# Sums of w_out's quarters: built a chunk of all four quarters at a time, stored from the sync queue

## The chip, the cores and the metric

The kernel runs on one core of one Trainium2 chip. The metric is the device time of one execution, in microseconds. The kernel before takes 1799.5 us (median of 3 runs, 1798.72 to 1800.11).

## The reference, cut to what matters

One decoder layer over 1024 positions of width 2048. After an RMSNorm and one input projection the columns split in two groups, and both groups' results meet in one output projection:

```
proj = rms_norm(x, norm_w) @ w_in
# group A: 8 heads x 128, gated delta rule in chunks of 64 (state recurrence)
# group B: 8 channel groups x 128, u * (W_s LN(v) + b) in chunks of 128, times silu(z)
mix = concatenate([o_a, o_b], -1) @ w_out        # (1024 x 2048) @ (2048 x 2048)
out = rms_norm(x + mix, final_norm_w)
```

The change concerns only how operands of the last product, `@ w_out`, are prepared.

## The kernel before, in words

The positions are worked in two halves of 512 (`hf` 0 and 1). In each half `group_a` projects eight heads in four pairs and runs the delta rule on them, and `group_b` projects v in three blocks of 256 columns (the `vb` matmuls, L790) and then u and z of eight channel groups (sixteen calls of `project`, 48 matmuls each: `acc`, L239 to L242). After both halves `out_phase` does the output projection. Every matmul operand is split in a high and a low part (`split`, L135 on ACT and L136 on DVE), so that three matmuls stand for one.

The output projection is done by a seven-product scheme of fast matrix multiplication on 2 x 2 blocks: `PRODUCTS` lists for each product which quarters of the left operand and of `w_out` are added. For products 0, 2 and 6 (`SUMS`) the sum or difference of two quarters of `w_out` is made beforehand, by `w_sums`, while group B runs, and kept in the DRAM tile `wc_d`; `out_phase` loads it from there. A quarter is 1024 x 1024, and is handled in chunks of 128 x 512 (256 KB): 2 column blocks `cb` by 8 row blocks `k` (`HK` is 8). So there are 3 x 16 = 48 sums in all. The first half makes the first 24 (all of product 0, and product 2 for `cb` 0), the second half the other 24.

`w_sums` makes one sum at a time: two loads issued by SP (`wsa` L839 into a buffer of tag `cv`, of which there are 3; `wsb` L840 into one of tag `bv`, of which there are 2), one DVE operation (L847), and one store issued by POOL (L848).

Two things set the order of the work. First, `w_sums` and most tasks of the heads are generators that are put on a list by `spawn` and advanced by `tick`, which the projections call after every six matmuls of 512 columns or twelve of 256. `yield n` lets n ticks pass. This gives the order in which instructions are written down. A call of `group_b` has 176 ticks: 48 in the three `vb` blocks and 128 in the sixteen projections. `w_sums` is spawned when group B's first weights are requested, four chunks of weights ahead of their matmuls and so about 8 ticks before the first of them. Second, the language then schedules the written instructions: it lays out each engine's queue before the program runs, by its own estimates of durations, with the order of writing as priority. An instruction whose inputs and buffers the estimate sees as free can be put in its queue well ahead of ones that are written before it. On the chip each queue runs in its fixed order, and an instruction at its head that waits holds those behind it.

Other places that the prediction's steps touch:

- The last pair of heads of a half (pair 3) finishes inside group B. Its state recurrence (`read` and `write`, L622 to L634) needs PE, DVE and PE again in turn. Then, one head after the other, come `at` (L650, PE), `o` (L651, DVE), a row of small operations, a scaling on POOL (L662), and a transposition through DRAM issued by POOL: four stores `swapo<-ut` (L431) and one load `ut<-swapo` (L434). The result is used at L673 on DVE, which frees a buffer of tag `ut`.
- `spatial` (L745, PE) fills one of the two PSUM banks of tag `gen`; L747 on DVE empties it into a buffer `s` of tag `ut`, of which there are 2. The `at` of the pair's second head needs a `gen` bank too.
- `w_chunk` issues the load of each weights chunk from SP (L186), into one of 3 buffers; its split parts have 4 buffers.

Of the kernel before, what the change touches and what calls it, by code (L numbers as in the profile page):

```python
# [8 lines left out]
F32 = mybir.dt.float32  # L9
# [3 lines left out]
ALU = mybir.AluOpType  # L13
# [4 lines left out]
P = 128  # L18
DM = 2048
SEQ = 1024  # L20
T = 512
# [10 lines left out]
def kernel(ctx, tc, x_tok, x_t, w_in, w_v0, w_vb, w_out, conv_w, norm_w, a_log, dt_bias,  # L32
                       hn_w, sgu_w, sgu_b, wsp_t, b_sp, fn_w, out):
    nc = tc.nc
# [5 lines left out]
    wk = pool("wk", bufs=2)  # L40
# [4 lines left out]
    def proj_bank(name):  # L45
        return ps.tile([P, T], F32, tag="proj", bufs=3, name=name)
# [71 lines left out]
    wc_d = dr.tile([3, 2, KT // 2, P, T], F32, name="wc_d", bufs=1)  # L118
# [64 lines left out]
    def w_chunk(src, shape, name, keep=None, raw=None, add=None):  # L183
        if raw is None:
            raw = wp.tile(shape, F32, tag="wr", bufs=3, name=f"wr{name}")
        nc.sync.dma_start(raw, src)  # L186
        if add:
            nc.vector.tensor_tensor(raw, raw, add[0], op=add[1])
        hi, lo = keep or (wp.tile(shape, F32R, tag="wh", name=f"wh{name}"), wp.tile(shape, F32R, tag="wl", name=f"wl{name}"))
        split(hi, lo, raw)  # L190
        return hi, lo
# [7 lines left out]
    def spawn(gen):  # L199
        n = next(gen, None)  # L200
        if n is not None:
            tasks.append([n, gen])

    def tick():
        for t_ in list(tasks):
            t_[0] -= 1
            if t_[0] <= 0:
                n = next(t_[1], None)
                if n is None:
                    tasks.remove(t_)  # L210
                else:
                    t_[0] = n
# [37 lines left out]
    def project(hf, ct, xs, done):  # L250

        st = {}
        for q in range(KT // KH):
            def mm(w, q=q):
                if q == 0:
                    st["acc"] = proj_bank(f"acc{hf}_{ct}")
                mm_chunk(st["acc"], w, xs, q)
                if q == KT // KH - 1:
                    done(st["acc"])
                    tick()  # L260
            yield (lambda q=q: w_tile(hf, ct, q)), mm
# [56 lines left out]
    def vsl(vn, t, c0, c1):  # L318

        return vn[c0 // T][:, t, c0 % T:c0 % T + c1 - c0]  # L320
# [135 lines left out]
    W_GATES = 12  # L456
    W_LN = 12
    W_EM = 5
    W_SUM0 = 18

    def task_k(hf, h, st, pr, acc):
        gt, hh = st["gt"], h % 2
# [255 lines left out]
    def task_ln(hf, vn, stt, sb):  # L718

        mv = sm.tile([P, NT, 2], F32, tag="mv", name=f"mv{hf}")  # L720
        rv = sm.tile([P, NT], F32, tag="rv", name=f"rv{hf}")
        va = sm.tile([P, NT], F32, tag="va", name=f"va{hf}")
        r4 = rstd[:, hf * NT:(hf + 1) * NT]
        for t in range(NT):
            nc.vector.bn_aggr(mv[:, t, :], stt[:, t])
        nc.vector.tensor_tensor(va, mv[:, :, 1], r4, op=ALU.mult)
        nc.vector.tensor_tensor(va, va, r4, op=ALU.mult)
        nc.vector.tensor_scalar(va, va, EPS, None, op0=ALU.add)
        rsqrt_(rv, va, [P, NT], f"v{hf}")
        nc.vector.tensor_tensor(rv, rv, r4, op=ALU.mult)  # L730
        for t in range(NT):
            v = vsl(vn, t, 0, T)
            nc.vector.tensor_scalar(v, v, mv[:, t, 0:1], rv[:, t:t + 1], op0=ALU.subtract, op1=ALU.mult)
        for t in range(NT):
            v = vsl(vn, t, T, 2 * T)
            nc.vector.tensor_scalar(v, v, mv[:, t, 0:1], rv[:, t:t + 1], op0=ALU.subtract, op1=ALU.mult)
        yield W_LN
        for g in range(2):
            spatial(hf, vn, sb, g)
            yield 1  # L740
# [12 lines left out]
    def task_u(hf, g, sb, acc):  # L753
        while g not in sb:
            yield 1
        nc.vector.tensor_tensor(sb[g], sb[g], acc, op=ALU.mult)

    def task_zb(hf, g, vn, sb, acc):
        za = scaled(acc, sb["rb"], f"zb{hf}_{g}")
        z = wk.tile([P, T], F32, tag="z", bufs=2, name=f"zb{hf}_{g}")  # L760
        nc.scalar.activation(z, za, AF.Silu)
        mx = wk.tile([P, T], F32, tag="kc", bufs=2, name=f"mb{hf}_{g}")
        nc.vector.tensor_tensor(mx, sb[g], z, op=ALU.mult)
        nc.sync.dma_start(mix_d[hf][H + g], mx)
        yield 1
        if g + 2 < NG:
            spatial(hf, vn, sb, g + 2)

    def group_b(hf, xs, st):

        env, sb = {}, {}
        units = [(n, cb, k) for n in SUMS for cb in range(2) for k in range(HK)]
        spawn(w_sums(units[hf * len(units) // 2:(hf + 1) * len(units) // 2]))
        for blk in range(1, 4):
            for k2 in range(KT // 2):
                def mm(w, blk=blk, k2=k2):
                    hi, lo = w
                    if blk == 1 and k2 == 0:
                        sb["rb"] = st["rb"]
                        env["vn"] = st["vn"] + [big.tile([P, NT, T], F32, tag="b8", name=f"vn{hf}_1")]  # L780
                    if k2 == 0:
                        env["acc"] = [proj_bank(f"vb{hf}_{blk}_{i}").rearrange("p (t c) -> p t c", c=256) for i in range(2)]
                    acc, vn = env["acc"], env["vn"]
                    for k in (2 * k2, 2 * k2 + 1):
                        xh, xl = xs[k]
                        for t in range(NT):
                            a, tsl = acc[t // 2][:, t % 2, :], slice(t * P, (t + 1) * P)
                            first, last = k == 0 and t % 2 == 0, k == KT - 1
                            for l, r, fl, sp_ in ((xh, hi, first, False), (xh, lo, False, False), (xl, hi, False, last)):
                                nc.tensor.matmul(a, l[:, tsl], r[:, k % 2, :], start=fl, stop=sp_, skip_group_check=True)  # L790
                        if k % 2 == 0:
                            tick()
                    if k2 == KT // 2 - 1:
                        for t in range(NT):
                            v = vsl(vn, t, blk * 256, (blk + 1) * 256)
                            nc.scalar.copy(v, acc[t // 2][:, t % 2, :])
                            nc.vector.bn_stats(st["st"][:, t, blk, :], v)
                        if blk == 3:
                            spawn(task_ln(hf, vn, st["st"], sb))
                    tick()  # L800
                yield (lambda blk=blk, k2=k2: w_chunk(w_vb[blk - 1, k2], [P, 2, 256], f"vb{hf}_{blk}_{k2}")), mm
        for g in range(NG):
            yield from project(hf, 4 * H + g, xs, lambda acc, g=g: spawn(task_u(hf, g, sb, acc)))
            yield from project(hf, 5 * H + g, xs, lambda acc, g=g: spawn(task_zb(hf, g, env["vn"], sb, acc)))
# [4 lines left out]
    HK = KT // 2  # L809
    PRODUCTS = (  # L810
# [7 lines left out]
    )  # L818


    SUMS = (0, 2, 6)
# [4 lines left out]
    op = {1: ALU.add, -1: ALU.subtract}  # L826

    def w_quarter(b, cb, k):

        return w_out[b[1] * 2 + cb, b[0] * HK + k]  # L830

    def w_sums(units):

        def load(u):
            n, cb, k = u
            a, b, _ = PRODUCTS[n][1]
            ta = wk.tile([P, 1, T], F32, tag="cv", bufs=3, name=f"wsa{n}_{cb}_{k}")
            tb = wk.tile([P, 1, T], F32, tag="bv", bufs=2, name=f"wsb{n}_{cb}_{k}")
            nc.sync.dma_start(ta, w_quarter(a, cb, k))  # L839
            nc.sync.dma_start(tb, w_quarter(b, cb, k))  # L840
            return ta, tb
        yield W_SUM0
        nxt = load(units[0])
        for i, (n, cb, k) in enumerate(units):
            (ta, tb), nxt = nxt, (load(units[i + 1]) if i + 1 < len(units) else None)
            yield 6
            nc.vector.tensor_tensor(ta, ta, tb, op=op[PRODUCTS[n][1][2]])  # L847
            nc.gpsimd.dma_start(wc_d[SUMS.index(n), cb, k], ta.rearrange("p o c -> p (o c)"))  # L848

    def out_phase():  # L850

# [209 lines left out]
```

## Time and profile before

| | |
|---|---|
| median of 3 runs | 1799.5 us |
| the profiled execution's own time | 1797.79 us |
| its span, first to last instruction | 1796.1 us |
| mean granted TensorE clock | 0.99 of full speed |
| PE busy | 1731.5 us, 96% of the span |
| DVE busy | 1271.1 us, 71% |
| ACT busy | 734.2 us, 41% |
| POOL busy | 290.2 us, 16% |
| moved by DMA | 284.27 MB, 158 GB/s over the span |

PE is the matmul engine. Its busy time bounds the kernel, so what another engine does costs time only where PE stands still for it, or runs at a lower granted clock after standing still. The stages follow each other: group A of the first half ends near 455 us, its group B near 735 us, group A of the second half near 1191 us, its group B near 1455 us, and the rest is the output projection.

### The profile page before, as it was taken

Reading aid. Unit: us, or ns where it says so; the run is one execution under the profiler, and the core shown is the slowest. Engines: PE = TensorE matmul, PEld = TensorE weight load, DVE = VectorE, ACT = ScalarE, POOL = GpSimd, SP = SyncE. Lnnn points to the kernel's source line nnn. Section 1 sums busy time; section 2 is a strip of 40 time slices with the busy share of each in tenths; the row PEclk is TensorE's granted clock in tenths of the full one; section 3 lists DMA queues with packets and bytes.
Section 4 is the critical chain, followed back from the end, with each engine's and each line's share of the span. In section 5 each row is a group of like instructions: output and inputs, shape, how many; then the busy total and the mean of one; then the engine's idle time right before and its main releaser. Section 6 shows DMA issues by size and latency. Waiting matters only on the chain.

```text
span 1796.1 us, 27540 instructions
## 1 busy us (share of the span) xinstructions
PE 1731.5 (96%) x9334; PEld 1458.4 (81%) x9334; DVE 1271.1 (71%) x2985; ACT 734.2 (41%) x1670; POOL 290.2 (16%) x362
## 2 busy tenths in 40 slices
PE   9999999999999799999999999999889999999997
PEld 8778787887997688887888888889778888778876
DVE  7798787987746633758879889793664345777885
ACT  7543544444333222636344444532422233333463
POOL 3210121211202300202012122120131000100121
PEclk9999999999999899999999999999999999999999
DMA  7455454364458744426453645443884367656774
GB/s 233 130 134 142 106 135 132 94 175 118 135 180 276 237 118 124 127 61 172 128 135 91 167 106 147 133 120 111 271 277 139 105 187 235 193 162 193 217 235 147
DMA packets 190429, 284.27 MB, mean 158 GB/s; under 512 B 38448, under 2 KB 71248, under 8 KB 190032
## 3 DMA queue, kind: packets, MB, share of 16 engines
q1 hardware_dynamic: 181760, 257.30, 49.8%
q0 software_dynamic: 8384, 25.21, 4.7%
q8 instruction: 73, 1.20, 0.3%
q14 instruction: 68, 0.56, 0.1%
q10 hardware_dynamic: 144, 0.01, 0.0%
HBM read 233.12 MB, written 49.32 MB: 157 GB/s over the span
## 4 chain that ended last, share of the span: by engine, by line
PE 66%; DVE 14%; DMA 11%; issue 4%; ACT 3%; POOL 1%; SPq 1%; DVEq 0%; ACTq 0%; POOLq 0%
PE acc L239 13%; PE acc L242 12%; PE acc L240 12%; PE vb L790 7%; PE oa L983 4%; PE oa L982 4%; PE oa L981 4%; DVE wl L136 2%; DMA wsb<-w_out 2%; DVE cv L414 2%; DMA xres<-x_tok 2%; DMA wc_d<-wsa 2%; DMA ar<-mix_d 1%; DMA pc<-swapk 1%; DVE fs L569 1%
## 5 line engine op out<-in xcount | busy, mean ns | idle before, releaser
L239 PE MATMUL acc<-xh,wh 128*128 128x512 f32 x1472 | 592.3, 402 | 1.0 <-ACT wh L135 1.0
L242 PE MATMUL acc<-xh,wl 128*128 128x512 f32 x1472 | 578.4, 393 | 5.4 <-DVE wl L136 5.2
L240 PE MATMUL acc<-xl,wh 128*128 128x512 f32 x1472 | 576.4, 392 | 0.0
L135 ACT CAST wh<-wr 128x512 fp32r<-128x512 f32 x368 | 226.2, 618 | 447.8 <-PE acc L240 285.0
L136 DVE TENSOR_TENSOR wl<-wr,wh 128x512 fp32r<-128x512 f32 x368 | 260.9, 712 | 139.1 <-ACT wh L135 137.6
L242 PEld LDWEIGHTS acc<-xh,wl 128*128 128x128 f32 x1472 | 277.8, 189 | 66.0 <-DVE wl L136 7.6
L239 PEld LDWEIGHTS acc<-xh,wh 128*128 128x128 f32 x1472 | 278.2, 189 | 58.1 <-issue 3.2
L240 PEld LDWEIGHTS acc<-xl,wh 128*128 128x128 f32 x1472 | 278.3, 189 | 51.8 <-issue 0.2
L982 PE MATMUL oa<-wlo,a 128*128 128x512 f32 x432 | 168.4, 390 | 3.5 <-DVE wlo L136 3.5
L981 PE MATMUL oa<-who,a 128*128 128x512 f32 x432 | 168.2, 389 | 0.8 <-ACT a L135 0.8
L983 PE MATMUL oa<-who,a 128*128 128x512 f32 x432 | 168.2, 389 | 0.7 <-DVE a L136 0.7
L414 DVE SCALAR_TENSOR_TENSOR cv<-pc,cw,cv 128x511 f32<-128x511 f32 (+1 forms) x144 | 108.7, 755 | 8.5 <-ACT cv L411 7.0
L790 PE MATMUL vb<-whvb,xh 128*128 128x256 f32 x384 | 111.1, 289 | 0.0
L790 PE MATMUL vb<-wlvb,xh 128*128 128x256 f32 x384 | 109.1, 284 | 0.0
L790 PE MATMUL vb<-whvb,xl 128*128 128x256 f32 x384 | 109.1, 284 | 0.0
L135 ACT CAST who<-wro 128x512 fp32r<-128x512 f32 x108 | 66.5, 617 | 89.1 <-PE oa L983 39.6
L982 PEld LDWEIGHTS oa<-wlo,a 128*128 128x128 f32 x432 | 81.1, 188 | 21.5 <-DVE wlo L136 4.7
L136 DVE TENSOR_TENSOR wlo<-wro,who 128x512 fp32r<-128x512 f32 x108 | 77.7, 723 | 29.1 <-ACT who L135 28.8
L981 PEld LDWEIGHTS oa<-who,a 128*128 128x128 f32 x432 | 81.1, 188 | 18.0 <-ACT a L135 1.3
L983 PEld LDWEIGHTS oa<-who,a 128*128 128x128 f32 x432 | 81.1, 188 | 17.9 <-DVE a L136 1.2
L569 DVE TENSOR_TENSOR fs<-fs,fst 32x31 f32<-32x31 f32 (+15 forms) x248 | 89.6, 361 | 4.1
L567 DVE TENSOR_TENSOR fst<-fs 32x31 f32<-32x31 f32 (+15 forms) x248 | 88.3, 356 | 4.2
(247 smaller groups left out, 2516.6 us busy)
## 6 DMA issues: line engine op xcount, KB each, us to landing
wr<-w_in SPq DMA_DIRECT2D x368, 256.0 KB, 3.3
wro<-w_out SPq DMA_DIRECT2D x64, 256.0 KB, 3.3
wsa<-w_out SPq DMA_DIRECT2D x48, 256.0 KB, 4.1
wrvb<-w_vb SPq DMA_DIRECT2D x48, 256.0 KB, 2.7
wsb<-w_out SPq DMA_DIRECT2D x48, 256.0 KB, 4.3
wc_d<-wsa POOLq DMA_DIRECT2D x48, 256.0 KB, 4.3
ar<-mix_d SPq DMA_DIRECT2D x48, 256.0 KB, 3.8
wro<-wc_d SPq DMA_DIRECT2D x48, 256.0 KB, 2.7
```

What stands on the lines that cost most here:

```text
L135: nc.scalar.copy(hi, src)
L136: nc.vector.tensor_tensor(lo, src, hi.bitcast(F32), op=ALU.subtract)
L239: nc.tensor.matmul(acc, hi[:, kk, :], xh, start=(k == 0), stop=False)
L240: nc.tensor.matmul(acc, hi[:, kk, :], xl, start=False, stop=(last and lo is None))
L242: nc.tensor.matmul(acc, lo[:, kk, :], xh, start=False, stop=last)
L414: nc.vector.scalar_tensor_tensor(cv[:, s:], acc[:, :T - s], w, cv[:, s:], op0=ALU.mult, op1=ALU.add)
L567: nc.vector.tensor_tensor(tv, bc(lu[:, k, k + 1:].unsqueeze(2), [32, n, m]), bc(xu[:, k:k + 1, 0:m], [32, n, m]), op=ALU.mult)
L569: nc.vector.tensor_tensor(xu[:, k + 1:, 0:m], xu[:, k + 1:, 0:m], tv, op=ALU.subtract)
L790: nc.tensor.matmul(a, l[:, tsl], r[:, k % 2, :], start=fl, stop=sp_, skip_group_check=True)
L981: nc.tensor.matmul(acc[t], ah[:, tsl], hi[:, 0, :], start=(k == 0), stop=False)
L982: nc.tensor.matmul(acc[t], ah[:, tsl], lo[:, 0, :], start=False, stop=False)
L983: nc.tensor.matmul(acc[t], al[:, tsl], hi[:, 0, :], start=False, stop=(k == HK - 1))
```

## The change

`w_sums` takes a list of (cb, k) instead of a list of sums. For each it loads the chunks of all four quarters (from SP, two into `cv` buffers and two into `bv` buffers), makes the three sums of that chunk in place on DVE, and stores the three results, now from SP. The first half does `cb` 0 and the second half `cb` 1, so each half still makes 24 sums. The first step is written 84 ticks after the spawn instead of 18, and the steps of a chunk lie 5, 1, 1 and 3 ticks apart.

```diff
-    W_SUM0 = 18
+    W_SUM0 = 84
...
-        units = [(n, cb, k) for n in SUMS for cb in range(2) for k in range(HK)]
-        spawn(w_sums(units[hf * len(units) // 2:(hf + 1) * len(units) // 2]))
+        spawn(w_sums([(hf, k) for k in range(HK)]))
...
-    def w_sums(units):
-
-        def load(u):
-            n, cb, k = u
-            a, b, _ = PRODUCTS[n][1]
-            ta = wk.tile([P, 1, T], F32, tag="cv", bufs=3, name=f"wsa{n}_{cb}_{k}")
-            tb = wk.tile([P, 1, T], F32, tag="bv", bufs=2, name=f"wsb{n}_{cb}_{k}")
-            nc.sync.dma_start(ta, w_quarter(a, cb, k))
-            nc.sync.dma_start(tb, w_quarter(b, cb, k))
-            return ta, tb
+    def w_sums(ck):
+
+        assert [PRODUCTS[n][1] for n in SUMS] == [((0, 1), (1, 1), -1), ((1, 0), (1, 1), 1), ((0, 0), (0, 1), 1)]
         yield W_SUM0
-        nxt = load(units[0])
-        for i, (n, cb, k) in enumerate(units):
-            (ta, tb), nxt = nxt, (load(units[i + 1]) if i + 1 < len(units) else None)
-            yield 6
-            nc.vector.tensor_tensor(ta, ta, tb, op=op[PRODUCTS[n][1][2]])
-            nc.gpsimd.dma_start(wc_d[SUMS.index(n), cb, k], ta.rearrange("p o c -> p (o c)"))
+        for cb, k in ck:
+            q = {}
+            for i, b in enumerate(((0, 0), (0, 1), (1, 0), (1, 1))):
+                q[b] = wk.tile([P, 1, T], F32, tag=("cv", "bv")[i // 2], bufs=(3, 2)[i // 2], name=f"ws{cb}_{k}_{i}")
+                nc.sync.dma_start(q[b], w_quarter(b, cb, k))
+            yield 5
+            nc.vector.tensor_tensor(q[0, 0], q[0, 0], q[0, 1], op=ALU.add)
+            nc.vector.tensor_tensor(q[0, 1], q[0, 1], q[1, 1], op=ALU.subtract)
+            yield 1
+            nc.vector.tensor_tensor(q[1, 0], q[1, 0], q[1, 1], op=ALU.add)
+            yield 1
+            for i, b in enumerate(((0, 1), (1, 0), (0, 0))):
+                nc.sync.dma_start(wc_d[i, cb, k], q[b].rearrange("p o c -> p (o c)"))
+            yield 3
```

## Rows read from the trace of the kernel before

**Rows 1.** Stretches: length, busy of PE, PEld, DVE, ACT, POOL; PEclk; DMA share, GB/s.

```profile
516.00:615.00 99.00, 82.33 (x451) 69.82 (x450) 60.41 (x151) 31.27 (x80) 23.90 (x36) 0.93 0.83 267
615.00:735.00 120.00, 120.00 (x547) 99.96 (x546) 48.74 (x69) 31.57 (x51) 9.39 (x8) 1.00 0.46 128
1252.00:1345.00 93.00, 80.83 (x447) 69.33 (x446) 58.97 (x148) 29.55 (x78) 22.69 (x35) 0.94 0.81 270
```

**Rows 2.** PE's waits, group B of the first half: total us, times, longest.

```profile
PE at L650 <- DVE s L747: 10.2, 1, 10.2
PE ds L633 <- DVE vz L625: 3.2, 4, 1.6
```

**Rows 3.** PE's longest wait, group B of the second half.

```profile
PE at L650 <- DVE s L747: 6.9, 1, 6.9
```

**Rows 4.** Timeline of SP's queue: start us, duration, what was issued.

```profile
421.42 1.66 SPq L839 DMA_DIRECT2D wsa<-w_out  x2
...
443.98 0.33 SPq L145 DMA_DIRECT2D xr<-x_t  x1
...
516.66 0.33 SPq L840 DMA_DIRECT2D wsb<-w_out  x1
```

**Rows 5.** Chain of waits, 560 to 600 us: start us, us, what.

```profile
578.00 1.47 POOL swapo L431 x2
...
580.55 0.56 POOL wc_d L848
...
584.63 2.88 issue
...
588.20 5.77 DMA ut<-swapo
...
595.35 0.76 DVE s L747
```

**Rows 6.** Timeline of POOL, second half; in brackets the idle time before.

```profile
1320.13 0.54 POOL L434 DMA_DIRECT2D ut<-swapo  x1 [1.60 <-DMA swapo<-ut]
```

**Rows 7.** DMA issues, 516 to 604 us: count, KB each, median us to landing.

```profile
wsb<-w_out SPq DMA_DIRECT2D x24, 256.0 KB, 4.4
wc_d<-wsa POOLq DMA_DIRECT2D x22, 256.0 KB, 4.3
...
swapo<-ut POOLq DMA_DIRECT2D x4, 64.0 KB, 5.0
ut<-swapo POOLq DMA_DIRECT2D x1, 256.0 KB, 5.8
```

**Rows 8.** DMA issues, 604 to 735 us.

```profile
swapo<-ut POOLq DMA_DIRECT2D x4, 64.0 KB, 3.7
ut<-swapo POOLq DMA_DIRECT2D x1, 256.0 KB, 3.0
```

**Rows 9.** DVE's waits ahead of the sums, whole kernel: total us, times, longest.

```profile
DVE wsa L847 <- DMA wsb<-w_out: 31.6, 18, 3.5
...
DVE wsa L847 <- DMA wsa<-w_out: 11.9, 7, 2.8
...
DVE wsa L847 <- issue: 3.6, 3, 2.2
```

**Rows 10.** The sums on DVE: duration ns min/median/max, first and last start.

```profile
L847 DVE TENSOR_TENSOR wsa<-wsa,wsb x48: 650/692/1766, 519.3 to 1340.4; 128x512 f32<-128x512 f32 x48
```

**Rows 11.** SP's waits ahead of the sums' loads, whole kernel.

```profile
SPq L839 <- DMA wc_d<-wsa: 60.0, 35, 4.3
```

**Rows 12.** Stretches of 3 us after PE's longest waits; columns as in rows 1.

```profile
596.00:599.00 3.00, 2.76 (x11) 2.59 (x12) 3.00 (x5) 0.00 (x0) 2.14 (x3) 0.50 0.75 250
599.00:602.00 3.00, 3.00 (x15) 2.57 (x14) 2.62 (x5) 2.13 (x9) 0.51 (x2) 0.70 0.72 182
...
1326.00:1329.00 3.00, 1.91 (x9) 1.94 (x10) 3.00 (x4) 0.34 (x1) 2.08 (x2) 0.50 0.88 277
1329.00:1332.00 3.00, 3.00 (x12) 2.44 (x12) 2.87 (x6) 1.44 (x6) 0.58 (x1) 0.62 0.48 118
```

## The prediction

> **What bounds the kernel now.** I read the engine table first: PE is busy 96% of the span, so a change to the sums can only gain where PE stands still or runs slow. Then I cut the span into stretches. In the first half's group B the sums stand between about 516 and 615 us, and PE is busy 82.33 of those 99 us; after them it is busy 120.00 of 120 us. In the second half it is busy 80.83 of 93 us while they run [rows 1]. So 16.7 + 12.2 = 28.8 us are lost beside the sums. PE's waits name two kinds. The larger is one wait in each half of `at` (L650) for `s` (L747), 10.2 and 6.9 us, 17.1 together [rows 2, 3]. The other 11.7 us are short waits in the state recurrence of pair 3, such as `ds` for `vz` [rows 2]. Third, the chain of waits tells what made `at` late in the first half: POOL's last swap store was issued by 579.47, two stores of sums to `wc_d` went before the swap's load, with 2.88 us of waiting for the next sum, the load started at 588.20 and took 5.77 us, and only then could DVE run L673 and L747 [rows 5]. In the second half the same load waited for the swap's own stores to land [rows 6]. Fourth, DVE's waits: it stood 31.6 + 11.9 + 3.6 = 47.1 us in front of sums whose loads had not landed [rows 9]. DVE runs in order, so whatever the recurrence wants next stands behind. Last, the granted clock: after the two long waits it is at the lower level for some us (0.50 in a stretch is 1.2 of 2.4 GHz). PE's busy time there, weighted with the missing clock, is 1.4 + 0.9 + 1.0 + 1.1 = 4.4 us [rows 12].
>
> **The start, W_SUM0.** In writing order the first sum moves from 10 to 76 ticks after group B's first matmul. But the queues do not follow writing order. The first loads of sums were issued at 421.42, before group B began, and an `x_t` load of the second half, written after the whole group, at 443.98; the first `bv` load followed at 516.66, when the heads' last use of that tag ended [rows 4]. So the loads went as soon as buffers were free, and those two tags have the same earlier users after the change. I therefore expect the sums to stay mostly where they are, beginning near 516 us: the later start by itself I put at nothing. Were it real, it would be worth the whole loss (second rival).
>
> **What is removed and added.** Loads fall from 96 to 64, stores stay 48, and sums stay 48 at 0.69 us on DVE [rows 10]: no DVE time goes. SP issues 112 transfers instead of 96, at 0.33 us each [rows 4] 5 us more, hidden because SP mostly stands waiting for buffers. Of 144 transfers of 256 KB, 22% go.
>
> **POOL no longer holds the swap.** Swap stores issued until 579.47 began their last at about 578.7; with the median 5.0 us to landing [rows 7] they land near 583.7, and the load could go then instead of at 588.20: 4.5 us in the first half, nothing in the second, where it waited for the landing anyway. Bounds: 0, if the load's other inputs are as late, and 7.6, from 580.6. I take 4.5.
>
> **The swap's transfers.** Beside the sums they took 5.0 and 5.8 us, after them 3.7 and 3.0 [rows 7, 8]: 4.1 us per half if all contention went, below nothing if the SP stores crowd it more. With a fifth of the transfers gone I take a third, 1.3 per half, 2.6 us.
>
> **DVE's waits in the swap's chain.** 48 sums cost 47.1 us of waiting, about 1 us each, and one comes every 4 us. Some three of them stand in the 12 us between `at` of the first head and its swap: 3 us per half. After the change the three sums of a chunk wait together. I take half, 1.5 per half, 3 us; bounds 0 to 6, and negative in the third rival.
>
> Together 4.5 + 2.6 + 3 = 10.1 of the 17.1 us. What is left of the waits is 2 to 5 us each, so I give back half of the clock's 4.4, 2.2 us.
>
> **The recurrence.** Its 11.7 us hang on how DVE's waits fall. Waits are fewer but longer, since a chunk's four loads are needed together. I take no change; bounds: all 11.7 gained, or as much lost again.
>
> **The new waits on SP.** A store on SP waits for its sum on DVE, and behind it stand the loads of `w_in` chunks. The longest such hold by `wc_d` so far was 4.3 us, 60.0 us over 35 times [rows 11], and PE did not wait for it: 547 matmuls in 120 us [rows 1] are 0.22 us each, a chunk of 12 takes 2.6, and four split buffers cover some 10 us. I take nothing. If that cover went (holds of over 10 us), each would cost PE the excess. The other new wait is that the next chunk's `bv` loads wait for a store to land, where before they waited only for the sum; that is the third rival.
>
> **The sum** is 12.3 us: 1785.5 against the profiled execution's 1797.8 (its span of 1796.1 and 1.7 around it). The median of the runs is 1.7 above that execution, so on that scale 1799.5 - 12.3 = 1787.2.
>
> **Rivals.** First, the swaps get all of the undisturbed times. For it: POOL's queue then carries no store of sums, and the swaps' times fell once these ended. Against it: loads from SP's own queue also took 4.4 us [rows 7], so the crowding is not of POOL's queue alone. It adds 8.2 - 2.6 = 5.6: 1781.6. The Trainium skill (DMA: Bandwidth & Descriptors, Queues, rings and completion order) says that each DMA engine goes round the queue rows packet by packet; by that rule transfers that have POOL's row to themselves would come out near these undisturbed times, against the third that I took from the share of transfers.
>
> Second, the late start is real. For it: the writing order, and that a sum yields to all that is written earlier. Against it: rows 4. Then nothing of the sums stands beside recurrence and swap; 28.8 + 4.4 go, and some 3 come back beside the later matmuls, where PE loses nothing now: 1799.5 - 30 = 1769.5.
>
> Third, slower. A chunk now has a longer loop through its `bv` buffers: four issues 1.3, landing 4.4, three sums 2.1, store issue 0.3, landing 4.3 [rows 4, 7, 10], 12.4 us, eight times 99 us, against the 90 that 24 single sums take now (519.3 to 609). If the queues are laid out as densely as now, the 9 us more per half become waits on DVE. Today 47.1 us of them cost PE 28.8 + 4.4 less the 4.5 of POOL, 0.6 of each us; the longer single waits outlast the recurrence's slack, so I reckon 0.8: 18 x 0.8 = 14.4 lost. Only the 4.5 and 2.6 remain against it: 1806.8. It decides from where DVE's waits ahead of sums exceed 47.1 + 7.1 / 0.8 = 56 us.
>
> Fourth, no change: the order laid out beforehand sees the freed POOL too and puts `at` that much earlier among the matmuls, so its wait stays: about 1798. For it: in the first half `at` came late against an order that already counted on some delay.
>
> **How the numbers follow.** My forecast gets 0.36, with its own range of 1783 to 1793; the swaps alone 0.12; the late start 0.12; slower 0.22; no change 0.18. The predicted time is the forecast's, 1787.2. The range 1770 to 1806 leaves out about half of the late start and half of the slower case, 0.17 in all. 0.2% is 3.6 us, about what a measurement of this kernel can tell from no change. Faster is 0.36 + 0.12 + 0.12 = 0.60, within it 0.18, slower 0.22.
>
> **What would show it.** Right: the changed kernel's `wsa`-like loads still begin near 421 and the `bv` ones near 516 us; POOL issues the swap's load within a us of the stores' landing; the two waits at L650 sum to about 7 us; DVE's waits ahead of the sums stay under 47 us. The late start shows as sums beginning after 570 us. Wrong: waits at L650 near 17 us still, DVE's waits over 56 us, or PE waiting for a `w_in` split because SP stood at a store. A loss outside the two stretches of rows 1, in the output projection say, is in no step above and would make the whole account wrong.

## The result, and the profile after

The changed kernel takes 1776.6 us (median of 4 runs, 1775.49 to 1781.86) against 1799.8 of the kernel before, timed beside it (1798.72 to 1807.08): a ratio of 0.9868, 95% interval 0.9836 to 0.9901. That is 23 us, about twice the forecast 12.3. It lies outside the forecast's own range of 1783 to 1793 and inside the whole range, 1770 to 1806, which was that wide for the sake of the rivals. Timed again later it gave 0.9873 [0.9849, 0.9898] (g3 below). The profiled execution has a span of 1775.6 us, 20.5 less than before, and the account below is made against that.

PE's stretches, in the columns of [rows 1]:

```profile
516.00:615.00 99.00, 92.88 (x495) 78.61 (x494) 65.06 (x157) 33.61 (x83) 14.98 (x16) 0.97 0.76 237
615.00:735.00 120.00, 118.67 (x544) 98.86 (x543) 53.37 (x78) 39.57 (x69) 10.58 (x11) 1.00 0.44 122
1240.00:1345.00 105.00, 99.37 (x549) 85.05 (x548) 68.12 (x161) 35.64 (x86) 16.06 (x16) 0.98 0.72 223
```

The sums still begin near 516 us, except the first sums of two chunks, whose loads go early (431.7 and 442.0 us), and still run beside the recurrence and the swap. In those stretches PE now loses 6.1 us of 99 and 5.6 of 105, 11.7 together against the 28.8 of [rows 1]: 17.1 us came back here. The third column from the right is the granted clock, 0.93 before and 0.97 now in the first stretch.

PE's waits, of the whole kernel (total us, times, longest), answering [rows 2, 3]:

```profile
PE at L650 <- DVE s L747: 9.5, 2, 5.0
PE ds L633 <- DVE vz L625: 6.2, 15, 0.9
```

The two long waits at L650 fell from 17.1 to 9.5. Most of the `ds` waits left lie outside the two stretches; inside group B of the first half there are 1.4 us, of 3.2 before.

DVE's waits ahead of the sums, whole kernel, answering [rows 9]:

```profile
DVE ws L842 <- DMA ws<-w_out: 16.5, 10, 3.4
...
DVE ws L841 <- DMA ws<-w_out: 4.4, 4, 1.5
```

20.9 us where it was 47.1. SP's waits around the sums, answering [rows 11]: ahead of the loads (L839) and, new, ahead of the stores (L847).

```profile
SPq L839 <- DMA wc_d<-ws: 24.5, 22, 2.7
SPq L847 <- DVE ws L842: 9.1, 9, 2.0
```

SP stands less for stores to land (24.5, was 60.0), and 48.1 us at the stores, all rows of L847 added up. Its timeline, answering [rows 4]:

```profile
419.99 2.38 SPq L839 DMA_DIRECT2D ws<-w_out  x2
...
443.15 0.38 SPq L145 DMA_DIRECT2D xr<-x_t  x1
...
514.75 0.33 SPq L839 DMA_DIRECT2D ws<-w_out  x1
```

The first loads go at 420, an `x_t` load of the second half at 443, and the load that waits for a `bv` buffer at 515, all within 2 us of before. The later place in writing order moved nothing.

The swap that `at` waits for, on POOL's timeline (in brackets the idle time before) and on the chain of waits, answering [rows 5]:

```profile
567.43 2.97 POOL L431 DMA_DIRECT2D swapo<-ut  x4 [1.47 <-DVE ut L426]
574.82 0.56 POOL L434 DMA_DIRECT2D ut<-swapo  x1 [4.42 <-DMA swapo<-ut]
```

```profile
569.66 4.58 DMA swapo<-ut
...
574.82 4.44 DMA ut<-swapo
...
580.15 0.76 DVE s L747
```

POOL stands 4.42 us for the swap's own stores, and its load is issued 0.6 us after the last landed; no store of a sum is between them any more. DMA issues of 516 to 604 us (count, KB each, median us to landing), answering [rows 7]:

```profile
ws<-w_out SPq DMA_DIRECT2D x26, 256.0 KB, 4.2
wc_d<-ws SPq DMA_DIRECT2D x22, 256.0 KB, 3.4
...
swapo<-ut POOLq DMA_DIRECT2D x8, 64.0 KB, 4.7
ut<-swapo POOLq DMA_DIRECT2D x2, 256.0 KB, 4.8
```

The swap's transfers are still crowded: 4.7 and 4.8, where it was 5.0 and 5.8 (both heads' swaps fall in this stretch now, only the first head's did before). But the store of a sum lands in 3.4 us where POOL's took 4.3. Last, the clock behind the two waits at L650, answering [rows 12]:

```profile
581.00:584.00 3.00, 2.96 (x11) 2.79 (x12) 1.36 (x3) 0.00 (x0) 1.62 (x1) 0.50 0.96 306
584.00:587.00 3.00, 3.00 (x11) 2.52 (x11) 2.89 (x5) 1.24 (x5) 0.04 (x1) 0.51 0.90 310
1306.00:1309.00 3.00, 1.38 (x6) 1.41 (x7) 3.00 (x5) 0.63 (x1) 1.44 (x1) 0.69 0.78 284
1309.00:1312.00 3.00, 3.00 (x15) 2.59 (x14) 2.55 (x4) 0.61 (x2) 0.20 (x1) 0.74 0.75 213
```

Busy time by missing clock is 1.5 + 1.5 + 0.4 + 0.8 = 4.2 us: waits of 4.5 and 5.0 us still put the clock to its lower level (0.50, 1.2 of 2.4 GHz), nearly as dearly as waits of 10.2 and 6.9 did (4.4). In the kernel before, though, there was a second place, after short waits of the recurrence, that the prediction did not count (kernel before, same columns):

```profile
542.00:545.00 3.00, 3.00 (x14) 2.63 (x14) 2.48 (x11) 1.79 (x5) 0.19 (x1) 0.63 0.67 238
545.00:548.00 3.00, 3.00 (x15) 2.44 (x14) 2.04 (x10) 0.88 (x4) 0.35 (x1) 0.80 0.87 236
1266.00:1269.00 3.00, 3.00 (x16) 3.00 (x17) 1.96 (x4) 1.25 (x4) 0.69 (x2) 0.57 0.87 279
1269.00:1272.00 3.00, 3.00 (x24) 3.00 (x24) 2.02 (x5) 1.28 (x3) 0.10 (x1) 0.86 0.95 337
```

1.1 + 0.6 + 1.3 + 0.4 = 3.4 us, and they are gone: between 516 and 563 us the changed kernel's clock is 1.00. In the kernel before, the clock had been at 0.50 since 591 us, while PE still stood, so part of the low stretch after the 10.2 us wait cost nothing.

The account of the 20.5 us, then: L650 7.6; the other waits in the two stretches 17.1 - 7.6 = 9.5; the clock 3.4 + 0.2 = 3.6; together 20.7. That this meets the 20.5 so closely is in part luck: outside the two stretches PE's standing fell by another 1.7 us, and the clock cost 1.5 more at one place near 96 us. Over the whole span, by the engine table, PE's standing fell by 18.8 us (64.6 to 45.8) and its busy time by 1.7 (1731.5 to 1729.8).

### The profile page after: what moved, and what is told of

It is laid out like the page before. It is cut to its first block, busy times and chain, and to the rows that moved or that the text cites. A ratio compares the mean times of both kernels' runs of the same rounds, so it can differ in the third digit from the quotient of the medians.

```text
span 1775.6 us, 27440 instructions
## 1 busy us (share of the span) xinstructions
PE 1729.8 (97%) x9334; PEld 1456.9 (82%) x9334; DVE 1265.6 (71%) x2985; ACT 736.2 (41%) x1670; POOL 261.6 (15%) x314
## 4 chain that ended last, share of the span: by engine, by line
PE 64%; DVE 16%; DMA 11%; issue 4%; ACT 3%; POOL 1%; SPq 1%; DVEq 0%; ACTq 0%; POOLq 0%
PE acc L239 12%; PE acc L242 12%; PE acc L240 12%; PE vb L789 7%; PE oa L983 3%; PE oa L982 3%; PE oa L981 3%; DVE wl L136 2%; DVE cv L414 2%; DMA ar<-mix_d 2%; DMA xres<-x_tok 2%; DMA ws<-w_out 2%; PE ds L633 1%; PE p L622 1%; DVE fst L567 1%
## 5 line engine op out<-in xcount | busy, mean ns | idle before, releaser
L242 PE MATMUL acc<-xh,wl 128*128 128x512 f32 x1472 | 577.6, 392 | 5.1 <-DVE wl L136 5.0
L135 ACT CAST wh<-wr 128x512 fp32r<-128x512 f32 x368 | 226.1, 618 | 447.2 <-PE acc L240 310.8
L136 DVE TENSOR_TENSOR wl<-wr,wh 128x512 fp32r<-128x512 f32 x368 | 256.7, 700 | 144.2 <-ACT wh L135 139.2
L242 PEld LDWEIGHTS acc<-xh,wl 128*128 128x128 f32 x1472 | 277.6, 189 | 64.9 <-DVE wl L136 6.6
L135 ACT CAST who<-wro 128x512 fp32r<-128x512 f32 x108 | 66.5, 618 | 86.4 <-PE oa L983 41.0
L136 DVE TENSOR_TENSOR wlo<-wro,who 128x512 fp32r<-128x512 f32 x108 | 77.9, 726 | 27.0 <-ACT who L135 26.7
```

The source lines that it names most:

```text
L135: nc.scalar.copy(hi, src)
L136: nc.vector.tensor_tensor(lo, src, hi.bitcast(F32), op=ALU.subtract)
L242: nc.tensor.matmul(acc, lo[:, kk, :], xh, start=False, stop=last)
```

## The experiments

Each kernel is one of the two with one thing altered; a ratio stands against the kernel before, timed beside it on the same chip. "Landing" is the median time from the issue of a `wc_d` store to its landing in 516 to 565 us, where recurrence and sums run side by side. "DVE" is what DVE stood in front of sums while the recurrence ran: from 516 us to pair 3's last `ds`, and from 1230 us to the same in the second half. These readings are of one execution each: after and g3 are the same kernel, and differ by 1.2 us in each of the two waits and by 0.3 in landing.

| run | base and edit | ratio [95%] | wait at L650 | DVE | landing |
|---|---|---|---|---|---|
| before | | 1 | 17.1 | 20.8 | 4.3 |
| after | | 0.9868 [0.9836, 0.9901] | 9.5 | 7.1 | 3.3 |
| e1 | after, start 18 | 0.9884 [0.9870, 0.9899] | 10.7 | 6.6 | 2.6 |
| e2 | after, stores by POOL | 0.9923 [0.9910, 0.9937] | 12.6 | 12.5 | 4.4 |
| e3 | before, stores by SP | 0.9883 [0.9864, 0.9903] | 9.1 | 9.9 | 3.3 |
| e4 | no sums | 0.9781 [0.9768, 0.9794] | 1.4 | | |
| f1 | before, 4 `cv` buffers | 0.9985 [0.9972, 0.9999] | 18.8 | 22.4 | 4.6 |
| f2 | before, stores by ACT | 1.0025 [1.0009, 1.0041] | 20.5 | 25.0 | 4.5 |
| f3 | before, o's swaps by SP | 1.0003 [0.9990, 1.0016] | 6.7 | 22.7 | 4.2 |
| f4 | after, true late start | 0.9856 [0.9833, 0.9878] | 1.0 | 0 | |
| g1 | before, loads and stores by POOL | 0.9927 [0.9903, 0.9951] | 14.9 | 17.1 | 4.2 |
| g2 | f4, sums on POOL | 0.9980 [0.9964, 0.9996] | 0.9 | | |
| g3 | after again | 0.9873 [0.9849, 0.9898] | 10.7 | 5.9 | 3.6 |
| h1 | before, SP stands at each sum | 0.9958 [0.9941, 0.9975] | 15.2 | 20.0 | 4.2 |

### The change taken apart: e1 to e4

e1, in the changed kernel:

```diff
-    W_SUM0 = 84
+    W_SUM0 = 18
```

> The changed kernel with the first sum written 18 ticks after the spawn again, all else as changed. Theory 'one wait for three' (DVE stands in front of the sums half as long because a chunk's three sums wait for one set of loads; the start is of no matter): ratio to the kernel before 0.984 to 0.990, DVE's waits ahead of the sums 18 to 26 us, sums still beginning near 516 us. Rival 'priority' (the late start lets the recurrence go first on DVE, and that gave the gain): ratio 0.993 or more, DVE's waits over 35 us, waits of ds for vz back at several us. Rival 'store path' expects the same as the first.

0.9884, 1782.4 us: as fast as the change within the intervals. Its waits of DVE ahead of sums are 12.1 + 11.2 + 1.4 = 24.7 us. Both 'one wait for three' and 'store path' had forecast this; 'priority' falls. In the changed kernel the number of the start is immaterial.

e2, in the changed kernel:

```diff
-                nc.sync.dma_start(wc_d[i, cb, k], ...)
+                nc.gpsimd.dma_start(wc_d[i, cb, k], ...)
```

> The changed kernel with the stores to wc_d issued by POOL again. 'One wait for three': only POOL's hold of the swap's load comes back, 4 to 5 us, and a little DMA time: ratio 0.989 to 0.993; recurrence waits stay near 2 us. Rival 'store path' (stores from SP land in 3.2 us instead of 4.2, so buffers come free and loads land sooner, and POOL is free): most of the gain goes, ratio 0.995 or more, DVE's waits ahead of the sums over 35 us. Rival 'priority': ratio as changed, 0.987.

0.9923, 1789.5 us: some 10 of the 23 us are given back, and 14 stay, although POOL issues the stores. Its PE waits:

```profile
PE at L650 <- DVE s L747: 12.6, 2, 6.9
...
PE ds L633 <- DVE vz L625: 9.7, 16, 2.1
```

Both kinds are longer again, while DVE's waits ahead of the sums over the whole kernel (21.6 + 4.7 + 2.1 = 28.4 us) rose little. The ratio is the one that 'one wait for three' had forecast, but the recurrence's waits did not stay near 2 us; 'store path' had expected 0.995 or more. In the stretch of the recurrence DVE stands 12.5 us for sums, between the change's 7.1 and the 20.8 of before.

e3, in the kernel before, and this edit alone:

```diff
-            nc.gpsimd.dma_start(wc_d[SUMS.index(n), cb, k], ...)
+            nc.sync.dma_start(wc_d[SUMS.index(n), cb, k], ...)
```

> The kernel before with its 48 stores to wc_d issued by SP instead of POOL, all else as before. 'One wait for three': 4 to 6 us gained at L650 in the first half and nothing in the recurrence: ratio 0.996 to 0.998. Rival 'store path': most of the gain, ratio 0.987 to 0.991, DVE's waits ahead of the sums under 30 us. Rival 'priority': 0.996 to 1.000.

0.9883, 1782.1 us, span 1775.6 as the changed kernel's: with all 96 loads, the old start and single sums it gives nearly all of the gain, as 'store path' had forecast. PE's waits, DVE's ahead of the sums, and SP's around them:

```profile
PE at L650 <- DVE s L747: 9.1, 2, 4.6
...
PE ds L633 <- DVE vz L625: 4.8, 15, 0.8
```

```profile
DVE wsa L847 <- DMA wsb<-w_out: 32.4, 24, 3.2
DVE wsa L847 <- issue: 11.0, 4, 5.3
DVE wsa L847 <- DMA wr<-w_in: 4.1, 2, 2.2
```

```profile
SPq L848 <- DVE wsa L847: 30.1, 23, 2.9
SPq L839 <- DMA wc_d<-wsa: 12.0, 6, 3.6
```

DVE waits 32.4 + 11.0 + 4.1, with a row of 0.7 in all 48.2 us, for its sums, as long as before (47.1) and not under 30 as 'store path' had it. And yet PE stands as little as in the changed kernel: it is busy 93.20 of the 99 us from 516 to 615. Where the waits lie tells why. These are DVE's waits ahead of the sums from 516 us to pair 3's last `ds`, before (to 561), in e3 (to 553) and in the changed kernel (to 554):

```profile
DVE wsa L847 <- DMA wsb<-w_out: 6.5, 5, 2.5
DVE wsa L847 <- DMA wsa<-w_out: 4.5, 3, 2.3
```

```profile
DVE wsa L847 <- DMA wsb<-w_out: 4.7, 3, 2.0
```

```profile
DVE ws L842 <- DMA ws<-w_out: 2.7, 2, 2.1
DVE ws L841 <- DMA ws<-w_out: 1.5, 1, 1.5
```

With two rows of 0.2 that is 11.2, 4.9 and 4.2 us; in e3 most of the other waits come after the recurrence. SP's standing has moved from the loads (60.0 us to 12.0) to the stores (30.1).

e4, in the changed kernel, makes no sums at all and so leaves out a part of the work:

```diff
-        spawn(w_sums([(hf, k) for k in range(HK)]))
...
-        src = w_quarter(...) if n not in SUMS else wc_d[...]
+        src = w_quarter(PRODUCTS[n][1][0], cb, k)
```

> The changed kernel without any sums of w_out: group B makes none, and the output projection loads one quarter where it took a sum (products 0, 2 and 6 are left without their second quarter). This is the ceiling of what any placing of the sums can gain. All theories: PE stands still in group B for under 3 us per half, and the time is 8 to 16 us under the changed kernel's: ratio 0.978 to 0.983. If it is above 0.985, the 13 us of PE's standing still that are left beside the sums have another cause.

0.9781, 1763.2 us, as forecast; PE stands 1.6 us in the first half's stretch and 1.0 in the second's. The ceiling of all that concerns the sums is some 39 us; the changed kernel still pays 13 to 16 of it.

### What about the stores' issuer counts: f1 to f3

f1 gives the kernel before a fourth buffer of tag `cv`, so that a load need not wait for the store two or three sums back. The number is changed at all six places that name the tag, those of the heads and of the output projection too; one of them:

```diff
-            ta = wk.tile([P, 1, T], F32, tag="cv", bufs=3, ...)
+            ta = wk.tile([P, 1, T], F32, tag="cv", bufs=4, ...)
```

> The kernel before with four buffers of tag cv instead of three, stores still from POOL. What is disputed now is why the store's queue alone gives nearly the whole gain (the run e3). Theory 'buffers come back': a load of the next sum waits on SP until an earlier store has landed, POOL's stores land later, and DVE then waits at the recurrence's cost; a fourth buffer takes that wait away. It expects SP's 60 us of waiting for wc_d to fall under 20, the waits of the recurrence to fall from 11.7 to under 5 us, L650 to stay near 17, ratio 0.992 to 0.996. Rival 'POOL's own doing' (the gain hangs on POOL not issuing these stores, whatever the buffers): recurrence waits stay near 11, ratio 0.998 or more.

0.9985, no gain worth the name. But SP still waited 45.3 us (30 times) ahead of L839 for landings, so the edit did not take away what it was meant to take away, and this run does not decide.

f2 and f3, each in the kernel before:

```diff
-            nc.gpsimd.dma_start(wc_d[SUMS.index(n), cb, k], ...)
+            nc.scalar.dma_start(wc_d[SUMS.index(n), cb, k], ...)
```

> The kernel before with its 48 stores to wc_d issued by ACT instead of POOL. 'Buffers come back': if they land in 3.2 to 3.9 us as from SP, the recurrence's waits fall under 5 us and the swap is not held: ratio 0.987 to 0.991. Rival 'pace' (a store on SP stands in the same queue as the loads and so holds back the next sums' loads until DVE is that far, which spaces the sums; ACT's queue doesn't): recurrence waits over 8 us, only L650 gains, ratio 0.993 to 0.997.

1.0025: slower, not faster. ACT's timeline shows a price of its own (in brackets the idle time before):

```profile
518.50 0.36 ACTq L848 DMA_DIRECT2D wc_d<-wsa  x1
519.12 0.59 ACT L609 COPY ut<-up 128x512 f32<-128x512 f32 x1 [3.46 <-DVE wsa L847]
```

A copy of the delta rule (L609) stands 3.46 us behind a store that waits for its sum. And the landing, 4.5 us, is like POOL's. Neither theory had this: L650 did not gain (20.5 us), and the `ds` waits rose to 16.0.

f3:

```diff
-            hd["ot"] = swap(y, ..., y, f"o{nm}", nc.gpsimd, True)
+            hd["ot"] = swap(y, ..., y, f"o{nm}", nc.sync, True)
```

> The kernel before with the transpositions of o through DRAM (four stores and a load per head) issued by SP instead of POOL; the stores to wc_d stay on POOL. It takes POOL's hold off the swap and nothing else. 'Buffers come back': L650's waits fall from 17 to 9 to 12 us, the recurrence's stay near 11: ratio 0.994 to 0.998. 'POOL's own doing' expects the same. If the ratio is 0.990 or less, the swap's hold alone was the whole matter.

1.0003. PE's waits:

```profile
PE ds L633 <- DVE vz L625: 9.4, 14, 2.1
PE p L622 <- DVE va L726: 7.8, 2, 4.5
PE acc L239 <- ACT wh L135: 7.5, 5, 2.1
...
PE at L650 <- DVE s L747: 6.7, 2, 3.4
```

L650 fell by 10 us, as if POOL's hold were the whole of it; but `w_in` chunks, queued on SP behind the swap, came late (the `acc` row, and one of 7.4 for L136), and the recurrence was no better. Nothing was gained, where both theories had forecast 0.994 to 0.998.

### The late start made real: f4 and g2

f4, in the changed kernel, lets the first chunk's loads wait for something that DVE writes late (`sb[2]`):

```diff
+        while 2 not in sb:
+            yield 1
...
+                if k == 0:
+                    nc.vector.tensor_copy(q[b][:, 0, 0:1], sb[2][:, 0:1])
```

> The changed kernel with a true late start: before the loads of the first chunk DVE writes one column of each of the four buffers from the third channel group's tile s (ready near 600 us), so that no sum can start before it. It is the late start that writing order alone did not bring. All theories that put the loss to sums beside recurrence and swap expect nearly the run without sums (ratio 0.978): 0.978 to 0.983, waits at L650 under 4 us, sums from about 600 to 700 us and PE not waiting for them. If it is 0.986 or more, the sums cost PE as much beside the plain projections.

0.9856, 1773.6 us: by its median the fastest of those that make the sums, not told apart from the change by the intervals, and short of the 0.978 to 0.983 that was forecast. In the first half its sums run from 597 to 671 us. The wait at L650 is 1.0 us, yet there is a new one, beside the later matmuls:

```profile
PE acc L242 <- DVE wl L136: 10.9, 8, 3.8
```

```profile
DVE ws L845 <- DMA ws<-w_out: 48.2, 15, 6.6
```

```profile
615.00:735.00 120.00, 115.57 (x525) 94.45 (x525) 66.52 (x98) 41.20 (x73) 11.93 (x11) 1.00 0.70 218
```

DVE stands in front of sums (48.2 us, and three smaller rows of 11.0, 6.7 and 0.7) with the split of `w_in` chunks (L136) behind it, and a part of the loss moves to where PE had lost nothing.

g2 takes that wait from DVE by adding on POOL, all three sums of a chunk alike:

```diff
-            nc.vector.tensor_tensor(q[0, 0], q[0, 0], q[0, 1], op=ALU.add)
+            nc.gpsimd.tensor_tensor(q[0, 0], q[0, 0], q[0, 1], op=ALU.add)
```

> The kernel with the true late start (sums held until the third channel group's tile s) and the 48 sums made by POOL instead of DVE, stores still from SP. In the gated run DVE stood 66 us in front of sums whose loads had not landed, and PE then waited 10.9 us for the split of w_in chunks that stood behind on DVE. If that is what is left of its loss, the wait moves to POOL, which has only s to scale there: L242's waits fall to about 5 us and the ratio to 0.979 to 0.984. Rival: SP, standing at a store for POOL's slower sum, holds the w_in loads, or POOL's standing delays s: ratio 0.986 or more.

0.998: some 22 us worse than f4. SP's waits:

```profile
SPq L851 <- POOL ws L845: 43.2, 14, 5.1
```

With two more rows like it (22.9 and 15.7) SP stands 82 us at stores for slow sums (1.4 to 1.5 us each on POOL). The `w_in` loads stand behind, and PE's waits for their split by ACT (L135) are 14.0 us in 16 times. That is the rival's account. It covers about half of the loss, though: PE's wait rows grew by 9 us (L135 by 13, L242 down by 4), its busy time by 13 (1729.2 to 1742.3), and no run tells why.

### Landing or pacing: g1 and h1

g1, in the kernel before, gives POOL the loads too:

```diff
-            nc.sync.dma_start(ta, w_quarter(a, cb, k))
-            nc.sync.dma_start(tb, w_quarter(b, cb, k))
+            nc.gpsimd.dma_start(ta, w_quarter(a, cb, k))
+            nc.gpsimd.dma_start(tb, w_quarter(b, cb, k))
```

> The kernel before with the sums' 96 loads issued by POOL as well as their 48 stores: all three transfers of a sum in one queue, but POOL's instead of SP's. What is disputed: in the recurrence's stretch a store from SP landed after 3.3 us and one from POOL or ACT after 4.3 to 4.5, with the loads at 4.0 to 4.3 in all. Theory 'same queue' (a store ahead of its successors' loads in one queue is served before them; in a queue of its own it shares the engines with them): stores land in 3.0 to 3.6 us. Rival 'SP's own quickness': stores still take 4.2 us or more. For the time both expect POOL's standing at loads and sums to hold the swap, so little of the gain: ratio 0.990 to 1.002; what tells is the landing.

0.9927: 13 us faster than before. The store's landing, by the DMA issues of 516 to 565 us:

```profile
wc_d<-wsa POOLq DMA_DIRECT2D x12, 256.0 KB, 4.2
```

So that a store lands sooner when loads and stores share a queue, whichever, is refuted. And more than half of e3's gain is to be had with late landings and with POOL still ahead of the swap (14.9 us at L650), when the engine that loads also stands at the store. Whether it is this, or that SP's queue is free for the `w_in` loads, g1 does not tell.

g3 is the changed kernel again:

> The changed kernel once more, unchanged, on the same chip and beside the same runs of the kernel before as the two others: ratio 0.984 to 0.990. All theories expect the same; it is there to place the late start on POOL against the change itself.

0.9873 and 1778.3 us, as the first time.

h1 is meant to tell pacing (SP issues the next loads only when a sum is done) from landing. In the kernel before, with POOL's stores left alone, SP stores 512 bytes of each sum to a scratch place, and so stands at the sum:

```diff
             nc.gpsimd.dma_start(wc_d[SUMS.index(n), cb, k], ...)
+            nc.sync.dma_start(pace_d[j:j + 1, :], ta[0:1, 0, 0:P])
```

> The kernel before, with its 48 stores of sums still issued by POOL; behind each, SyncE also stores the first 128 numbers (512 bytes) of the same sum to a scratch place, 24.6 kB in all. So SyncE stands at each sum as it did where the stores themselves were its own (30.1 us in 23 waits), while the full store still lands as POOL's do. Theory 'pacing' (what spares the recurrence is that SyncE issues the next load only once the sum is done): ratio 0.986 to 0.991, 1778 to 1786 us, PE's waits at L650 about 9 us and for ds about 5, with landings of wc_d at 4.2 us or more. Theory 'landing' (it is the store's quicker landing, 3.3 us against 4.3, or POOL's own part in it): ratio 0.997 to 1.003, 1794 to 1805 us, waits at L650 about 17 us, wc_d at 4.2 us or more still.

0.9958, between the two forecasts. SP's and PE's waits (lines stand one or three further on):

```profile
SPq L840 <- DMA wc_d<-wsa: 31.6, 27, 3.0
SPq L851 <- DVE wsa L848: 30.9, 22, 3.6
SPq L840 <- DMA pace_d<-wsa: 16.1, 13, 3.3
```

```profile
PE at L651 <- DVE s L748: 15.2, 2, 8.4
PE p L623 <- DVE state L635: 8.2, 5, 4.1
```

SP stands at the sums as in e3 (30.9 us in 22 waits, e3 30.1 in 23), and of e3's 1.17% only 0.42% is there: 7.6 of 21 us, about a third. Waits of `ds` fell to 7.7 us, but two of 4.1 and 3.4 us for `state` came in, and DVE's waits in the recurrence stayed (20.0, before 20.8). The small stores have a cost of their own (SP waits 16.1 us for them to land), so pacing may be worth more than the third. What h1 leaves out is not the landing alone: POOL still has the sums' stores ahead of the swap's load, where e3 has freed it (the load goes 0.6 us after the swap's stores landed, as in the changed kernel).

## Why the prediction was right in direction and half in size

**Where it begins.** "the later start by itself I put at nothing": shown, by SP's timeline and by e1. The argument that the loads follow their buffers was right. f4 shows what a real late start does: 1773.6, against 1769.5 for that rival.

**POOL's hold of the swap's load.** Shown, and of the size forecast: the load now goes 0.6 us after the landing, and from the first swap store to the load it is 7.4 us in the first half where it was 11.7, 4.3 less (forecast 4.5). Three stores of sums stood in between before, issued at 580.54, 584.07 and 587.53, not two as the prediction reads. But f3, which ends the hold by another way, gains nothing in all, so a shorter wait at L650 is worth something only if its cure costs nothing elsewhere.

**The two waits at L650.** 7.6 us came back of 17.1 (5.7 and 1.9 by half), forecast 10.1; 9.5 are left, where 7 were foretold. The way from the first head's `at` to the second's shortened by 7.0 and 2.4 us, so the mechanism was right and the size nearly. The term that fell short is the swap's transfers, 2.6 us: the load took 4.4 us instead of 5.8 in the first half, but 5.5 instead of 4.7 in the second. The first rival, undisturbed swaps, fell: with 22 stores out of POOL's queue they took 4.7 and 4.8 us, far from the 3.7 and 3.0 of [rows 8]. The Trainium skill (DMA: Bandwidth & Descriptors, Queues, rings and completion order) has each DMA engine take turns between queue rows; the prediction drew from it that transfers alone in POOL's row would come near the undisturbed times, and here they did not.

**The clock.** "half of the clock's 4.4" was expected back at L650; 0.2 came. The 3.4 us that did come back lay elsewhere, behind the recurrence's waits, where the prediction had counted none.

**The step that failed** is "The recurrence. ... I take no change": it gave 9.5 us and the 3.4 of clock, more than L650 did, and near the upper of its bounds. The prediction said itself that these waits hang on DVE's; what failed is that it put DVE's waits there at no change, "fewer but longer", from a total over the kernel. While the recurrence ran, DVE's waits for sums fell from 20.8 to 7.1 us, and the longest in the first half from 2.5 to 2.1 us. The total misleads: e3 gains the same at 48.2 as the change at 20.9, and f4 is fastest at 66.6. So the point at which the third rival was to decide (56 us in all) means nothing either, and that rival fell by its own loop: a chunk takes 10.6 us (523.07 to 597.56 in seven steps), not 12.4.

**What counts instead.** Who issues the stores is enough: e3 alone gives the change's gain, and the only gain that the prediction ascribed to the issuer was the 4.5 us of the swap's load. But it is not needed for all of it: e2, with POOL's stores, keeps 14 of 23 us. The column "DVE" puts the runs nearly in the order of their ratios: 5.9 to 9.9 us at 0.9868 to 0.9884, 12.5 at 0.9923, 17.1 at 0.9927, 20.0 at 0.9958, and 20.8 to 25.0 at 0.9985 to 1.0025 (f4, with none there, has its waits beside the later matmuls). It is thus borne out, by the runs side by side, that the gain goes by how long DVE stands in front of sums while the recurrence needs it; no run alters that alone.

Why stores from SP shorten these waits is not shown. The landing is one candidate: in the table's stretch a store landed in 2.6 to 3.6 us where the ratio is 0.9868 to 0.9884 (after, e1, e3, g3), and in 4.2 or more where it is 0.9923 to 1.0025 (e2, f1, f2, f3, g1, h1), and a buffer waits for this landing before its next load. But over all 48 stores the gap is smaller, 3.1 to 3.7 us against 3.9 to 4.6, with e2 (3.9) near e3 (3.7), and between 565 and 615 us it is gone (3.9 to 4.2 against 4.0 to 4.7). The others are pacing, a third of e3's gain by h1, and POOL's freedom for the swap. The Trainium skill (Trainium Kernel Development and Optimization, Key Constraints) says that issuing DMAs from several engines only saves the sequencer's issue time. By that e3 would have moved 0.54 us per store off POOL, which is busy 16% of the span. It moved the kernel by 21 us.

**Fewer transfers.** With SP's stores a third fewer loads and sums by the chunk are worth no more than the 0.15% between e3 and the change, inside both intervals. With POOL's stores the same is worth 0.77% (e2 against before). The two halves of the change are two ways to much the same gain, and do not add up.

**SP's new waits cost nothing.** Right for the change: SP stands 48.1 us at the stores, and PE's `acc` waits for split chunks of 5.0 us are those of the kernel without sums (e4, 5.1). g2 shows the limit: with 82 us at stores, PE waits 14 us for splits of `w_in` chunks.

**The range.** That the measured time lay inside it is not to the credit of the sum. The range reached below 1783 us for the undisturbed swaps and the late start, and neither happened.

Open: why a store issued by SP lands sooner early in the stretch and not late in it; and how e3's gain divides between landing, pacing and POOL's freedom.

## What to carry to other kernels

Which queue issues a store is a choice with a price: try the engine that issues the next loads into the same buffers, alone, before judging a change of the transfers' number. A total of waits on an off-path engine says little; read its waits in the stretch in which a dependent chain (here the recurrence) alternates between that engine and PE. And a bound taken from "all of it gained" deserves weight when the step changes everything that the lost time stands beside.

## What the hardware showed that was not expected

- The 256 KB stores from SBUF landed in 2.6 to 3.6 us when SP issued them, 4.2 to 4.6 from POOL and 4.5 from ACT, in 516 to 565 us (medians of 11 to 14; before and e3, with the same loads, 4.3 and 3.3); over all 48 in 3.1 to 3.7, 3.9 to 4.6 and 4.4. DVE's own operations were not slower beside POOL's issues: the sums took 691 ns each in 516 to 563 us with POOL's stores and 688 with SP's.
- A wait of 4.5 us on PE cost as much clock afterwards (2.9 us over 581 to 587) as one of 10.2 us did before (2.3 over [rows 12]'s first two stretches), where the clock had gone down 5 us before PE went on.
- An addition of 128x512 took 1.4 to 1.5 us on POOL, 0.69 on DVE.
